# Modulation products of a four-layer diffusion step, in bursts of four feature tiles with a load one burst ahead

## The chip, the cores and the metric

The kernel runs on one core of a Trainium2 chip. The metric is device time in microseconds of one execution; of several runs the median counts. All times below come from the times of the kernel before and from one profiled execution of it.

## What is computed

The reference is one inference step of a four-layer backbone on 512 latent tokens and 128 context tokens, 1024 features wide. Layer i uses another attention (neighbourhood, sliding window, low rank, grouped), and every layer has the same frame. What concerns this case is the adaptive normalisation: each layer takes six vectors of 1024 numbers from a product of the conditioning vector with a 1024 x 6144 matrix.

```python
def adaln(cond, w_mod, b_mod):
    m = jax.nn.silu(cond) @ w_mod + b_mod
    return [t[:, None, :] for t in jnp.split(m, 6, axis=-1)]

def modulate(h, shift, scale):
    return h * (1 + scale) + shift

# a layer, with (shift1, scale1, gate1, shift2, scale2, gate2) = adaln(...)
# x = x + gate1 * mixer(modulate(rms_norm(x, norm1_g), shift1, scale1))
# x = x + gate2 * swiglu(modulate(rms_norm(x, norm2_g), shift2, scale2))
def swiglu(h, w_gate, w_up, w_down):
    return (jax.nn.silu(h @ w_gate) * (h @ w_up)) @ w_down
```

There are two conditioning vectors (latents and context), so the modulation is a product with two rows: little arithmetic, and 24 MB of weights a layer that are read once.

## The kernel before

Activations lie feature-major: eight feature tiles of 128 rows by 640 tokens. The large products are done to float32's accuracy from a high and a low part of each operand: a weight block of 128 x 512 is loaded (`raw`, 256 KB, four places in turn), ScalarE copies its high part (`whi`), VectorE or GpSimd subtracts to get the low part (`wlo`), and TensorE makes three products of each pair. In the feed-forward part the accumulators are called `big`, and the gate and up products go by seven block products (Strassen), whose sums of weights are `sum`. In attention `S` holds the scores, `tp` transposes, and `sm` the rest. `sm` also holds the modulation's accumulator in every phase.

The modulation of the next layer is made as a filler beside other work. The generator `mod_part` makes 4 w columns: for each of the eight feature tiles k it loads a strip of the matrix (128 x 4 w, `rawm`) and makes four products of 32 rows side by side in the array, then it yields; a ninth step copies the accumulator out (`modev`), puts the values into columns with a small product by `sel`, and adds the bias. Layer 0's own columns 2048 to 6144 are made in its attention with w = 128, and their strips lie in the `raw` places of the weights. All others use w = 256, strips of 512 KB in two buffers of their own (`rawm`): layer 1's in the feed-forward part of layer 0, layer 2's in the attention (two thirds) and feed-forward part (one third) of layer 1, layer 3's in the feed-forward part of layer 2. Layer 3 makes none. The first layer's first 2048 columns have a function of their own, `mod_first`, which stays.

Where a step stands in the program is set by `job` and `tick` in attention (so many steps spread over the 16 units) and by `fill` in the feed-forward part: `EDGE` steps after the output product, some after each gate or up product, and the last `EDGE` ones at the end by `flush`. The order on each engine is then set by the tile framework's scheduler, which goes by priority and a simulated timeline: it may draw a later instruction forward where it believes an engine to be idle. All weight, modulation and key loads are issued by SyncE (SP) in one order; `k<-k` copies keys from one half of the partitions to the other, `bias` and `craw` are loads for attention.

A passage that this text calls the edge is the beginning of a feed-forward part: output product, second normalisation (`make_b`, on VectorE, lines 630 to 651), and the first gate and up products. The remainder is called the interior.

Of the kernel before, what the change touches and what calls it, by code (L numbers as in the profile page):

```python
# [37 lines left out]
# feature tiles whose token halves go one after the other at the end of a phase, and steps of modulation kept for there  # L38
LAST, EDGE = 2, 9
# units of attention by which a group's products, normalisation and pairs are ahead  # L40
# [4 lines left out]
# ---------------------------------------------------------------- layout of the weights  # L45
# [5 lines left out]
def weight_plan():  # L51
    """(key, features tiles, columns, builder) of every weight of a product, in the order of use."""
# [59 lines left out]
# columns (one value a partition) and rows (one value a column, the same in every partition)  # L112
# [29 lines left out]
def na_bias(rpb):  # L142
    """Bias and validity of the three kinds of query block: [16 heads, 128 queries, 3, 384]."""
# [24 lines left out]
def to_perm(a):  # L168
    """Latent tokens from (row, column) order to (column // 8, row, column % 8) order, first axis."""
    return a.reshape(8, 8, 8, *a.shape[1:]).swapaxes(0, 1).reshape(a.shape)  # L170
# [89 lines left out]
# ---------------------------------------------------------------- the kernel  # L260
class Net:
# [5 lines left out]
    # -- small helpers  # L267
# [3 lines left out]
    def alt(self, out, in_, share=0.5):  # L271
        """A copy, on the scalar engine for a share of the calls and on the vector engine for the others."""
        self.flip += share
        if self.flip >= 1:
            self.flip -= 1
            self.nc.scalar.copy(out, in_)
        else:
            self.nc.vector.tensor_copy(out, in_)

    def banks(self, kind):  # L280
        """The accumulators of a phase: name -> (banks of each, number)."""
# [8 lines left out]
    def weights(self, key, part=None):  # L290
        """The blocks of a weight, or one of them, on chip in two parts: for each feature tile (high, low) [128, n]."""
# [14 lines left out]
    def two(self, raw, eng):  # L306
        """The two parts of a block."""
# [5 lines left out]
    def slots(self, more):  # L313
        """The places of blocks and of their parts, in turn; the feed-forward phase has some more of them."""
# [23 lines left out]
    # -- the whole  # L338
# [13 lines left out]
    def constants(self):  # L352
        nc, a, cp = self.nc, self.a, self.cp
        # two columns a feature tile: a product takes these and 30 more, whose rows of the result nobody reads
# [22 lines left out]
    # -- modulation: silu(cond) @ w_mod + b_mod, as columns  # L377
# [6 lines left out]
    def mod_first(self, b, pool):  # L384
        """The first layer's shift and scale of feature tiles 2 b and 2 b + 1."""
# [22 lines left out]
    def mod_part(self, L, c0, w, pool, tag=None, bufs=1):  # L408
        """Columns c0 to c0 + 4 w - 1 of the layer's modulation: four products side by side in the array."""
        nc = self.nc  # L410
        mod, moda = self.mod_tiles(L)
        acc = self.ps()
        for k in range(ND):
            raw = pool.tile([P, 4 * w], F32, tag=tag, name=tag, bufs=bufs) if pool else self.slot("raw")
            nc.sync.dma_start(raw, self.a["wmod"][L, k * P:(k + 1) * P, c0:c0 + 4 * w])
            for j in range(4):
                self.mm(acc[32 * j:32 * j + 32, :w], self.cond[:, 2 * k:2 * k + 32], raw[:, j * w:(j + 1) * w], k == 0, k == ND - 1)
            yield
        ev = (pool or self.wp).tile([P, w], F32, tag="modev", name="modev")
# [16 lines left out]
    def mod_parts(self, L, c0, c1, *args):  # L436
        w = args[0]
        self.mod_done[L] = c1
        for c in range(c0, c1, 4 * w):
            yield from self.mod_part(L, c, *args)  # L440

    def fill(self, n):
        """n steps of the work that waits for idle time of the tensor engine."""
# [15 lines left out]
    # -- normalisation  # L459
    def stat(self, pool, d, halves=(0, 1), src=None):  # L460
        """Adds the squares of feature tile d; after the last one, makes 1 / rms of every token."""
# [51 lines left out]
    # -- products  # L513
    def mm3(self, out, x, w, start, stop):
        """out += x.T @ w to float32's accuracy, from parts of 12 bits."""
# [4 lines left out]
    def proj_first(self, key, n, evac):  # L520
        """Token-major product of h, the features outermost: five accumulators of n columns."""
# [13 lines left out]
    def proj(self, key, n, evac):  # L535
        """Token-major product of h, a step for each tile of tokens."""
# [10 lines left out]
    def feat(self, halves, ws, acts, L, i, d):  # L547
        """Feature-major product, x += gate * w.T @ act over the list of feature tiles: halves is {half: bank}."""
# [7 lines left out]
    def halves_first(self, weights, acts, L, i, n, after, step=None):  # L556
        """feat for all feature tiles; for the last n, the first half of the tokens goes first."""
# [14 lines left out]
    def residual(self, L, i, d, halves):  # L572
        """x += gate * y for one feature tile of y, or a half of it: halves is {half: y}."""
# [6 lines left out]
    # -- products by seven block products (Strassen, Winograd's form)  # L580
# [3 lines left out]
    def scaled(self, pool, L, halves, d, raws):  # L584
        """A feature tile of x (or a half of it) by its scale, for make_b."""
# [13 lines left out]
    def make_b(self, pool, L, B, raws):  # L599
        """The second normalisation: the quarters of h that the seven block products take and their sums, all in two  # L600
        parts: B[name] = [(high, low) of feature tile i of the half's four]. A step for each feature tile of the first
# [526 lines left out]


class Full(Attn):  # L1130
    """All the latents against the latents and the cache."""

    def blocks(self, g, pr, hf, u):
        net = self.net
# [598 lines left out]
```

## Time and profile before

| | us |
|---|---|
| median of 3 runs | 3285.33 |
| lowest, highest | 3277.95, 3286.36 |
| span of the profiled execution | 3285.3 |
| TensorE busy with matmuls | 3123.6 |
| VectorE busy | 2155.9 |
| ScalarE busy | 1527.9 |
| GpSimd busy | 1264.1 |

The profiled execution is as long as the median run to a tenth of a microsecond, so terms worked out from it can be set against the median as they stand. In the profile a float32 matmul of the modulation appears as two records, so one step of four products is a row of x8, and four steps together are x32. A matmul's duration overlaps the next one's, so what a group costs is read from the start of the instruction before it to the start of the one behind it. `128*32` is the part of the array that an instruction uses (rows by columns).

### The profile page before, as it was taken

How to read it: one execution, taken by the hardware profiler on the slowest of the kernel's cores; microseconds unless marked ns; L12 is line 12 of the kernel's file. 1: busy time of each engine (PE TensorE's matmuls, PEld its weight loads, DVE VectorE, ACT ScalarE, POOL GpSimd, SP SyncE). 2: the span in 40 equal slices, each digit the busy share in tenths (PEclk: the TensorE clock that was granted, in tenths of full speed). 3: DMA queues.
4: the chain of work that ended last, by engine and by line, in shares of the span. 5: the costliest groups of instructions: out<-in, count | busy, mean ns of one | idle time of the engine just before them, and what ended most of it. 6: DMA issues, size and time to landing. Idle time of an engine off the chain costs nothing. (4 is left out here: it accounts for less than half of the span.)

```text
span 3285.3 us, 58663 instructions
## 1 busy us (share of the span) xinstructions
PE 3123.6 (95%) x22157; PEld 2847.0 (87%) x22157; DVE 2155.9 (66%) x4167; ACT 1527.9 (47%) x3300; POOL 1264.1 (38%) x1175
## 2 busy tenths in 40 slices
PE   8999989999999999999987999999999999899999
PEld 6997879999887788999976778899998878799999
DVE  5554496666576768667668766865765765867665
ACT  4555453433346755334346765433433576534332
POOL 2442362322244444323234545432322553633322
PEclk9998999999999999999998999999999999899999
DMA  7346542433433343222211223423333111122222
GB/s 236 100 119 195 184 155 86 127 104 117 126 122 98 105 135 105 76 84 83 88 45 40 64 64 120 135 86 119 117 102 122 53 32 29 55 87 76 80 82 83
DMA packets 168251, 331.50 MB, mean 101 GB/s; under 512 B 19616, under 2 KB 49696, under 8 KB 167968
## 3 DMA queue, kind: packets, MB, share of 16 engines
q1 hardware_dynamic: 164800, 323.47, 32.6%
q8 instruction: 175, 2.87, 0.4%
q10 hardware_dynamic: 3168, 4.28, 0.4%
q14 instruction: 108, 0.88, 0.1%
HBM read 303.86 MB, written 4.28 MB: 94 GB/s over the span
## 5 line engine op out<-in xcount | busy, mean ns | idle before, releaser
L269 PE MATMUL big<-hh,whi 128*128 128x320 f32 x2720 | 829.9, 315 | 24.7 <-ACT hh L619 8.5
L269 PE MATMUL big<-hl,whi 128*128 128x320 f32 x2720 | 832.1, 312 | 6.7 <-DVE hl L623 4.6
L269 PE MATMUL big<-hh,wlo 128*128 128x320 f32 x2720 | 824.1, 311 | 0.9 <-DVE wlo L310 0.9
L309 ACT CAST whi<-raw 128x512 fp32r<-128x512 f32 (+3 forms) x668 | 387.7, 586 | 674.1 <-PE big L269 431.8
L310 DVE TENSOR_TENSOR wlo<-raw,whi 128x512 fp32r<-128x512 f32 (+1 forms) x504 | 432.5, 862 | 201.6 <-ACT whi L309 198.5
L269 PEld LDWEIGHTS big<-hh,whi 128*128 128x128 f32 x2720 | 508.4, 190 | 53.9 <-DVE sv L696 13.6
L269 PEld LDWEIGHTS big<-hl,whi 128*128 128x128 f32 x2720 | 511.7, 190 | 20.9 <-DVE hl L623 10.8
L269 PEld LDWEIGHTS big<-hh,wlo 128*128 128x128 f32 x2720 | 510.1, 189 | 2.9 <-DVE wlo L310 2.9
L310 DVE TENSOR_TENSOR wlo<-sum,whi 128x512 fp32r<-128x512 f32 x336 | 302.0, 903 | 73.3 <-ACT whi L309 68.4
L309 ACT CAST whi<-sum 128x512 fp32r<-128x512 f32 x352 | 215.8, 618 | 272.5 <-PE big L269 226.4
L269 PE MATMUL big<-al,whi 128*128 128x320 f32 x1408 | 335.9, 311 | 3.2 <-POOL al L582 3.2
L310 POOL TENSOR_TENSOR wlo<-raw,whi 128x512 fp32r<-128x512 f32 (+2 forms) x164 | 223.4, 1374 | 294.4 <-ACT whi L309 266.5
L269 PE MATMUL big<-ah,whi 128*128 128x320 f32 x1408 | 333.8, 312 | 1.2 <-ACT ah L734 1.2
L269 PE MATMUL big<-ah,wlo 128*128 128x320 f32 x1408 | 333.4, 310 | 0.0
L1018 POOL TENSOR_SCALAR p<-p,st 128x640 f32<-128x640 f32 (+2 forms) x256 | 201.2, 790 | 315.7 <-DVE st L1017 227.9
L709 POOL TENSOR_TENSOR y<-y,sv 128x320 f32<-128x320 f32 x132 | 146.7, 1118 | 354.0 <-DVE sv L696 300.8
L670 POOL TENSOR_TENSOR sum<-raw,sum 128x512 f32<-128x512 f32 x88 | 124.0, 1409 | 410.1 <-ACT whi L309 206.2
L670 POOL TENSOR_TENSOR sum<-raw 128x512 f32<-128x512 f32 x88 | 127.5, 1449 | 364.7 <-DMA raw<-in_wall 180.6
L577 DVE SCALAR_TENSOR_TENSOR x<-big,mod,x 128x320 f32<-128x320 f32 (+2 forms) x480 | 182.4, 432 | 117.4 <-PE big L269 116.8
L269 PEld LDWEIGHTS big<-al,whi 128*128 128x128 f32 x1408 | 240.2, 189 | 6.5 <-POOL al L582 3.7
L269 PEld LDWEIGHTS big<-ah,whi 128*128 128x128 f32 x1408 | 238.3, 188 | 8.0 <-issue 2.5
L269 PEld LDWEIGHTS big<-ah,wlo 128*128 128x128 f32 x1408 | 239.6, 189 | 0.2
(264 smaller groups left out, 6169.2 us busy)
## 6 DMA issues: line engine op xcount, KB each, us to landing
raw<-in_wall SPq DMA_DIRECT2D x644, 256.0 KB, 2.7
rawm<-in_wmod SPq DMA_DIRECT2D x144, 512.0 KB, 4.3
raw<-in_wmod SPq DMA_DIRECT2D x96, 256.0 KB, 4.5
k<-k SPq DMA_DIRECT2D x38, 384.0 KB, 4.4
raw<-in_wall SPq DMA_DIRECT2D x96, 128.0 KB, 2.2
bias<-in_nabias SPq DMA_DIRECT2D x16, 576.0 KB, 5.5
qpe<-pes SPq DMA_DIRECT2D x56, 80.0 KB, 2.1
out_y<-x ACTq DMA_DIRECT2D x8, 320.0 KB, 2.2
```

The source lines that it names most:

```text
L269: self.nc.tensor.matmul(out, lhsT=lhsT, rhs=rhs, start=start, stop=stop, skip_group_check=True)
L309: self.nc.scalar.copy(hi, raw)
L310: eng.tensor_tensor(lo, raw, hi.bitcast(F32), ALU.subtract)
L577: self.last = self.nc.vector.scalar_tensor_tensor(xs, halves[b][:, p0:p1], self.mcol(L, i, d, c), xs, ALU.mult, ALU.add)
L670: eng.tensor_tensor(raw[n], raw[x], raw[y], op)
L709: nc.gpsimd.tensor_tensor(y, y, v, ALU.mult)
L1018: nc.gpsimd.tensor_scalar(p, p, rd, 1.0, ALU.mult, ALU.mult)
```

## The change

`mod_parts` no longer loads a strip inside each step. It keeps a list of bursts, each of four feature tiles of one group of 1024 columns. `mod_load` issues the four loads of the next burst into four buffers `rawm`; a step then makes all 16 products of the burst that is on chip, issues the next burst's four loads into the same buffers, and yields. The second burst of a group goes on to the copy and the bias in the same step. So a group of 1024 columns takes two steps in place of nine, and there is one more step at the very start that only loads. Layer 0's columns are now made with w = 256 in buffers of the attention's pool, so they no longer use the weights' `raw` places, and their products are 256 columns wide in place of 128. `EDGE` goes from 9 to 2, and the counts of steps are adapted. A setting that shrinks a scratch area of DMA descriptors makes room for the buffers.

```diff
-LAST, EDGE = 2, 9
+LAST, EDGE = 2, 2
+MODW, BURST = 256, 4
...
-    def mod_part(self, L, c0, w, pool, tag=None, bufs=1):
-        nc = self.nc
+    def mod_part(self, L, c0, pool):
+        nc, w = self.nc, MODW
         mod, moda = self.mod_tiles(L)
         acc = self.ps()
-        for k in range(ND):
-            raw = pool.tile([P, 4 * w], F32, tag=tag, name=tag, bufs=bufs) if pool else self.slot("raw")
-            nc.sync.dma_start(raw, self.a["wmod"][L, k * P:(k + 1) * P, c0:c0 + 4 * w])
-            for j in range(4):
-                self.mm(acc[32 * j:32 * j + 32, :w], self.cond[:, 2 * k:2 * k + 32], raw[:, j * w:(j + 1) * w], k == 0, k == ND - 1)
-            yield
-        ev = (pool or self.wp).tile([P, w], F32, tag="modev", name="modev")
+        for k0 in range(0, ND, BURST):
+            raws = self.mod_raw.pop(0)
+            for k, raw in zip(range(k0, k0 + BURST), raws):
+                for j in range(4):
+                    self.mm(acc[32 * j:32 * j + 32, :w], self.cond[:, 2 * k:2 * k + 32], raw[:, j * w:(j + 1) * w], k == 0,
+                            k == ND - 1)
+            self.mod_load(pool)
+            if k0 + BURST < ND:
+                yield
+        ev = pool.tile([P, w], F32, tag="modev", name="modev")
...
-    def mod_parts(self, L, c0, c1, *args):
-        w = args[0]
+    def mod_load(self, pool):
+        if self.mod_todo:
+            L, c, k0 = self.mod_todo.pop(0)
+            raws = []
+            for k in range(k0, k0 + BURST):
+                raws.append(pool.tile([P, 4 * MODW], F32, tag="rawm", name="rawm", bufs=BURST))
+                self.nc.sync.dma_start(raws[-1], self.a["wmod"][L, k * P:(k + 1) * P, c:c + 4 * MODW])
+            self.mod_raw.append(raws)
+    def mod_parts(self, L, c0, c1, pool):
         self.mod_done[L] = c1
-        for c in range(c0, c1, 4 * w):
-            yield from self.mod_part(L, c, *args)
+        cs = range(c0, c1, 4 * MODW)
+        self.mod_todo, self.mod_raw = [(L, c, k0) for c in cs for k0 in range(0, ND, BURST)], []
+        self.mod_load(pool)
+        yield
+        for c in cs:
+            yield from self.mod_part(L, c, pool)
...
-                todo = (6144 - c0) // 1024 * 9 - 2 * EDGE
-                self.filler = [self.mod_parts(L + 1, c0, 6144, 256, fp, "rawm", 2)]
+                todo = (6144 - c0) // (4 * MODW) * (ND // BURST) + 1 - 2 * EDGE
+                self.filler = [self.mod_parts(L + 1, c0, 6144, fp)]
...
-                self.job(net.mod_parts(2, 0, 4096, 256, self.ap, "rawm", 2), 36, 0, 16)
+                self.job(net.mod_parts(2, 0, 4096, self.ap), 9, 0, 16)
...
-            self.job(net.mod_parts(0, 2048, 6144, 128, None), 72, 7, 16)
+            self.job(net.mod_parts(0, 2048, 6144, self.ap), 9, 7, 16)
...
-    nc = bacc.Bacc("TRN2", target_bir_lowering=False, num_devices=1)
+    nc = bacc.Bacc("TRN2", target_bir_lowering=False, num_devices=1, dynamic_dma_scratch_size=1024)
```

On TensorE, in the last down product of layer 0's feed-forward part, where the trace of before has a wait at 881 us, the order before has two steps together between products by `ah` and `al` (the gated activations' parts):

```order
L269 MATMUL big<-ah,whi 128x320
L269 MATMUL big<-al,whi 128x320
L269 MATMUL big<-ah,wlo 128x320
L269 MATMUL big<-ah,whi 128x320 x6
L269 MATMUL sm<-rawm,cond 32x256 x8
L269 MATMUL big<-al,whi 128x320 x2
L269 MATMUL big<-ah,wlo 128x320 x2
```

and after, at the tenth of the twelve bursts of that part, the four steps of a burst stand in one row:

```order
L271 MATMUL big<-hh,whi 128x320
L271 MATMUL big<-hl,whi 128x320
L271 MATMUL big<-hh,wlo 128x320
L271 MATMUL sm<-rawm,cond 32x256 x16
L271 MATMUL big<-ah,whi 128x320 x2
L271 MATMUL big<-al,whi 128x320 x2
```

What moved is that 16 products stand between the same two large ones, where there were 8.

On SP, in the second half of layer 0's attention, loads of single strips before (`raw<-in_wmod`, in the weights' places) alternate with weights, biases and key copies:

```order
L299 DMA raw<-in_wall 128x512
L415 DMA raw<-in_wmod 128x512 x6
L299 DMA raw<-in_wall 128x512
L415 DMA raw<-in_wmod 128x512 x3
L1298 DMA bias<-in_nabias 128x1152
L299 DMA raw<-in_wall 128x512
L415 DMA raw<-in_wmod 128x512 x2
L983 DMA k<-k 64x1536 x2
L1298 DMA bias<-in_nabias 128x1152
```

and after:

```order
L301 DMA raw<-in_wall 128x512 x2
L448 DMA rawm<-in_wmod 128x1024 x4
L1317 DMA bias<-in_nabias 128x1152
L448 DMA rawm<-in_wmod 128x1024 x2
L301 DMA raw<-in_wall 128x512
L448 DMA rawm<-in_wmod 128x1024
L1002 DMA k<-k 64x1536 x2
L1317 DMA bias<-in_nabias 128x1152
```

What moved is that strips of twice the size go in rows of up to four, and weights have their places to themselves.

At the edge of layer 0's feed-forward part SP has before:

```order
L415 DMA rawm<-in_wmod 128x1024 x3
L665 DMA raw<-in_wall 128x512 x2
L415 DMA rawm<-in_wmod 128x1024
L665 DMA raw<-in_wall 128x512
L415 DMA rawm<-in_wmod 128x1024 x8
L665 DMA raw<-in_wall 128x512
L415 DMA rawm<-in_wmod 128x1024 x2
```

and after:

```order
L448 DMA rawm<-in_wmod 128x1024 x4
L684 DMA raw<-in_wall 128x512
L448 DMA rawm<-in_wmod 128x1024
L684 DMA raw<-in_wall 128x512
L448 DMA rawm<-in_wmod 128x1024
L684 DMA raw<-in_wall 128x512
L448 DMA rawm<-in_wmod 128x1024 x12
L684 DMA raw<-in_wall 128x512
```

What moved is that more strips stand at the edge, up to 12 in a row without a weight between them.

## Rows read from the trace of the kernel before

**Rows 1.** The page's first part: engine, busy us (share of the span), instructions.
```profile
PE 3123.6 (95%) x22157; PEld 2847.0 (87%) x22157; DVE 2155.9 (66%) x4167; ACT 1527.9 (47%) x3300; POOL 1264.1 (38%) x1175
```

**Rows 2.** Windows: attention of layer 0, interior, attention of layer 1, interior of layer 2.
```profile
core 0: us, PE busy (x) PEld busy (x) DVE busy (x) ACT busy (x) POOL busy (x), PEclk, DMA share, GB/s
...
240.00:391.00 151.00, 137.62 (x1366) 114.16 (x1365) 66.68 (x200) 70.88 (x188) 38.98 (x58) 0.92 0.59 184
...
480.00:910.00 430.00, 426.44 (x2962) 405.66 (x2960) 268.47 (x442) 154.68 (x284) 127.87 (x92) 1.00 0.35 110
910.00:1183.00 273.00, 260.08 (x1953) 212.27 (x1949) 187.13 (x526) 163.54 (x454) 118.80 (x141) 0.98 0.34 106
...
2090.00:2518.00 428.00, 424.44 (x2955) 405.89 (x2954) 268.92 (x443) 153.79 (x285) 128.87 (x94) 1.00 0.35 108
```

**Rows 3.** The tile `rawm` over the whole span: ns min/median/max, first and last start.
```profile
L269 PE MATMUL sm<-rawm,cond x1152: 379/379/637, 415.7 to 2517.5; 128*32 128x256 f32 x192
...
DMA to landing us min/median/max: 3.4/4.3/7.8
```

**Rows 4.** Timeline of TensorE, layer 0's interior (start, length): two steps, one step.
```profile
701.39 0.31 PE L269 MATMUL big<-hh,wlo 128*128 128x320 f32 x1
701.63 1.07 PE L269 MATMUL sm<-rawm,cond 128*32 128x256 f32 x16
702.63 0.42 PE L269 MATMUL big<-hh,whi 128*128 128x320 f32 x1
...
863.17 0.31 PE L269 MATMUL big<-hl,whi 128*128 128x320 f32 x1
863.32 0.31 PE L269 MATMUL big<-hh,wlo 128*128 128x320 f32 x1
863.56 0.64 PE L269 MATMUL sm<-rawm,cond 128*32 128x256 f32 x8
864.13 0.56 PE L269 MATMUL big<-ah,whi 128*128 128x320 f32 x2
```

**Rows 5.** Timeline of TensorE, layer 0's attention: four steps of 128 columns, one step.
```profile
276.52 1.08 PE L269 MATMUL sm<-raw,cond 128*32 128x128 f32 x32
...
290.46 0.43 PE L269 MATMUL sm<-raw,cond 128*32 128x128 f32 x8
```

**Rows 6.** TensorE's waits (us, times, longest) in 240:391, 480:910, 910:1183, 2090:2520.
```profile
PE sm L269 <- DMA raw<-in_wmod: 6.7, 7, 1.9
...
PE sm L269 <- DMA rawm<-in_wmod: 3.0, 2, 2.4
...
PE sm L269 <- DMA rawm<-in_wmod: 2.8, 3, 1.8
...
PE sm L269 <- DMA rawm<-in_wmod: 2.2, 2, 1.7
```

**Rows 7.** Lines 630 and 582 at the edges of layers 2 and 3; window of layer 2's.
```profile
L630 DVE TENSOR_TENSOR raw<-raw,rstd x16: 476/479/1584, 2036.8 to 2063.4; 128x320 f32<-128x320 f32 x16
L582 DVE TENSOR_TENSOR hl<-raw,hh x4: 476/478/1143, 2058.4 to 2069.5; 128x320 fp32r<-128x320 f32 x4
...
L630 DVE TENSOR_TENSOR raw<-raw,rstd x16: 476/480/1582, 2828.6 to 2853.0; 128x320 f32<-128x320 f32 x16
L582 DVE TENSOR_TENSOR hl<-raw,hh x4: 477/1150/1158, 2847.9 to 2862.1; 128x320 fp32r<-128x320 f32 x4
...
2028.00:2086.00 58.00, 49.43 (x372) 36.08 (x371) 53.25 (x88) 35.71 (x77) 34.23 (x27) 0.97 0.65 211
```

**Rows 8.** Windows of layer 0's attention, columns as in Rows 2: full queues, and behind them.
```profile
276.00:280.00 4.00, 4.00 (x57) 3.52 (x55) 2.03 (x9) 2.78 (x9) 0.59 (x1) 1.00 1.05 334
...
304.00:308.00 4.00, 2.96 (x21) 2.52 (x20) 0.42 (x1) 1.86 (x4) 1.28 (x1) 1.00 1.05 248
308.00:312.00 4.00, 2.54 (x22) 1.85 (x20) 1.23 (x3) 0.00 (x0) 0.00 (x0) 1.00 1.06 208
312.00:316.00 4.00, 3.10 (x20) 2.53 (x20) 0.97 (x3) 1.16 (x3) 0.00 (x0) 0.52 0.63 192
316.00:320.00 4.00, 4.00 (x25) 3.50 (x25) 1.51 (x9) 2.45 (x8) 2.72 (x4) 0.50 0.20 68
```

## The prediction

> **What bounds the kernel now.** I read the page first: TensorE is busy with matmuls for 95% of the span, the next engine, VectorE, for 66% [rows 1]. Then the windows by stage. In the interiors of layers 0 and 2, TensorE is busy 426.4 of 430 and 424.4 of 428 us [rows 2]: there is no hole, and whatever it does not have to do shortens the stage. In the two attentions that carry modulation it is idle 13.4 us of 151 (layer 0) and 12.9 of 273 (layer 1) [rows 2]: mostly bound by TensorE, with waits in between. The edges are another case. The second normalisation, from the first product of line 630 to the last subtraction of line 582, takes 2036.8 to 2069.5 = 32.7 us in layer 2, with modulation beside it, and 2828.6 to 2862.1 = 33.5 us in layer 3, which has none; VectorE is busy 53.3 of 58 us there and TensorE 49.4 [rows 7]. So at an edge VectorE sets the time and modulation is free up to the 8 to 9 us that TensorE has left.
>
> Then the modulation itself, which in float32 is 1152 matmul records of `rawm` (a few are missing) and runs from 416 to 2518 us [rows 3]. The timeline tells what a step costs. One step alone: the large product before it starts at 863.32, the one behind at 864.13, 0.81 us apart, where two large ones follow each other after 0.15 us (863.17, 863.32); so the step takes 0.66 us. Two steps in one row: 701.39 to 702.63, 1.24 us, so 1.09 for both [rows 4]. A further step costs 0.43 us, and the going over to the 128 x 32 part of the array and back 0.23 us. For strips of 128 columns, eight records last 0.43 us and 32 last 1.08 us, so a further step costs 0.65 / 3 = 0.22 us [rows 5]; the switch I take as the same 0.23.
>
> **The change, part by part.** *Fewer switches.* I counted in both orders the rows of modulation products that stand between other TensorE instructions, and the steps in them (products over four, rounded up, since a piece of one to three products takes as long as four side by side: a large share of the rows are such pieces, and the bursts are broken up by the scheduler too). Interior of layer 0: 28 rows and 39 steps before, 12 and 26 after: 28 x 0.23 + 39 x 0.43 = 23.2 us before, 12 x 0.23 + 26 x 0.43 = 13.9 after, -9.3. Interior of layer 2: 24 and 33 before, 12 and 26 after: 19.7 to 13.9, -5.8. Attention of layer 1: 33 and 39 before, 25 and 43 after: 24.4 to 24.2, -0.1 (here the bursts are cut into many pieces). Attention of layer 3: a leftover of 0.7 goes. Attention of layer 0, with 0.22 a step before: 45 rows and 73 steps of 128 columns, 26.4 us, to 22 rows and 39 steps of 256 columns, 21.8 us: -4.6. All of this lies on an engine that is full or nearly so. Sum: -20.5 us.
>
> By the Trainium skill, TensorEngine Tiling (Array Packing), Key Properties, a change of the tiling mode drains TensorE; with the drain of some 175 ns that TensorE: Matmul & The Clock Gate gives under Single matmul latency, a switch would be estimated at 0.18 us in place of 0.23, and the sum at some -17 in place of -20.5. The measured 0.23 decides.
>
> *Steps moved to the edges.* Part of the interiors' gain is that work goes to the edges: 18 to 27 steps and 15 to 18 rows in layer 0, 19 to 27 and 16 to 18 in layer 2, 17 to 16 and 14 to 9 in layer 1. On TensorE that is 4.6 + 3.9 - 1.6 = +6.9 us. What hides it is VectorE's chain of the second normalisation, which took the same 33 us with and without modulation, and TensorE's 8.6 idle us in 58 [rows 7]. The loads: some eight strips more of 0.52 MB each add 4.2 MB to 211 GB/s x 58 us = 12.2 MB, together 283 GB/s; the queues have moved 334 GB/s [rows 8]. So I charge 0, and 6.9 us if the cover is gone.
>
> *Waits for strips.* TensorE itself waits for modulation strips 6.7 us in layer 0's attention, 3.0 in layer 0's interior, 2.8 in layer 1's attention and 2.2 in layer 2's interior [rows 6]. Two buffers and a landing of 4.3 us (3.4 to 7.8) [rows 3] leave little lead. With a burst ahead a strip has the time between two bursts: in layer 0's interior the closest pair is 56 large products apart, 56 x 0.146 = 8.2 us, and 2.1 MB at 334 GB/s take 6.3 us. So these waits can go. But a wait can also come back, since four loads wait together for the same burst on SP. Bounds for the four: all 14.7 us gained, or as much lost again. In the two interiors, whose loads have few neighbours (DMA share 0.35 [rows 2]), I take 3 of the 5.2; in the attentions, where weights and key copies go through the same queue, 1.3 of 9.5. Sum -4.3.
>
> *SP.* Every burst has four loads that wait for TensorE to have read the buffers; behind them on SP wait weights, biases and key copies. The number of bytes is the same, and before, too, each load waited for a matmul and had the same neighbours; in layer 0's attention weights now have their own places, which can only help them. I charge 0, and the price if this is wrong is the second rival. *The rest:* the small products, the copies and the bias stay; in layer 0 their number halves, off the path. The accumulator `sm` is held over two steps in place of nine: not priced, and in the lower end of the range.
>
> Sum: -20.5 + 0 - 4.3 = -24.8 us. The profiled execution took 3285.3 us, as much as the median, so the forecast is **3260 us**.
>
> **The rivals.** *Everything goes.* If all waits for strips go as well, it is -20.5 - 14.7, and with the idle time and low clock behind some of them (0.50 for 4 us after the long waits of layer 0's attention [rows 8]) some 6 more: -41, 3244 us. For it: four loads in flight in place of two. Against: VectorE or a weight is often late next.
>
> *The queue jams, and it is slower.* In layer 0's attention the queues are full from 304 to 312 us (share 1.05 and 1.06, 248 and 208 GB/s), TensorE idles 1.0, 1.5 and 0.9 us in three slices of 4 us, and then runs at a clock of 0.52 and 0.50, the lower of its two levels (1.2 GHz), for 8 us [rows 8], which loses half of what it could have done in them: 3.4 + 4.0 = 7.4 us for one jam, and some 10 with a slow slice more on either side. Such a jam comes where strips, a bias and key copies are asked for at once, and a burst puts 2.1 MB in front of them in one piece. There are 16 bursts in the two attentions that carry modulation. Were five of them to jam anew, it would be -24.8 + 50 = +25, 3310 us. It decides from three and a half new jams (35 us, 10 over the gain). DMA: Bandwidth & Descriptors of the Trainium skill, Queues, rings and completion order, says that descriptors of one ring are consumed in order, so a small copy issued behind a burst waits for it; that is the mechanism here, and the full slices agree with it. Against: the same bytes went through the same queue before, and layer 1's attention has a DMA share of 0.34 [rows 2].
>
> *It comes to nothing.* The edges are not covered (+6.9), the waits only move to other places (0), and in the attentions the switches saved are swallowed by waits on softmax: -9.3 - 5.8 + 6.9 = -8 us, 3277 us. For it: the idle 13 us in each attention show that TensorE is not alone on the path there.
>
> That the change does not do what it says, because the scheduler cuts the bursts up, is in the counts above; in layer 1's attention it is the case.
>
> **How the numbers follow.** Forecast (3250 to 3272) 0.60; everything goes 0.12; comes to nothing 0.15; jam 0.13. About 0.3%, 10 us, can be told from no change. Faster by more (below 3275.5) are the first two, 0.72; the same is the third, 0.15; slower the jam, 0.13. The range holds the forecast, everything that goes (3243 and up) and the case of nothing up to its uncovered end, 3288; the jam is left out.
>
> **What would show it.** In the profile after: in the interiors rows of x32 at 2.0 us in place of x8 at 0.66, their stretches some 9 and 6 us shorter; the waits for `rawm` there gone; the edges as long as before, line 630 to line 582 in 33 us. Layer 0's attention 5 to 8 us shorter, layer 1's as before. I am wrong if the edges grow by more than 3 us each (strips too late for the rows of 12 loads), if waits on key copies or weights grow in an attention, or if a stretch of low clock stands behind bursts.

## The result and the profile after

The changed kernel takes 3258.52 us (median; 3253.98 to 3266.37), beside 3286.36 us for the kernel before on the same chip: ratio 0.9917, 95% interval 0.9894 to 0.994. That is 27.8 us less; the forecast was 3260 and 25 less. The profiled execution of the changed kernel took 3255.87 us (its span is 3254.1), 2.7 below the median, so single stages of it are read with care below.

The page's first part, engine, busy us (share of the span) and instructions, answers to [rows 1]:

```profile
PE 3104.7 (95%) x21901; PEld 2843.0 (87%) x21901; DVE 2166.9 (67%) x4166; ACT 1527.7 (47%) x3296; POOL 1263.1 (39%) x1175
```

TensorE is busy 18.9 us less, and no other engine has become a bound. The windows by stage (columns as in [rows 2]: attention of layer 0 from 240 us, interior of layer 0, attention of layer 1, interior of layer 2):

```profile
240.00:380.00 140.00, 129.81 (x1077) 103.91 (x1076) 70.27 (x199) 70.37 (x185) 40.89 (x56) 0.95 0.62 194
469.00:884.00 415.00, 412.95 (x2886) 402.39 (x2884) 270.47 (x440) 153.84 (x284) 127.87 (x93) 1.00 0.32 100
884.00:1161.00 277.00, 263.81 (x1946) 216.18 (x1945) 190.95 (x527) 164.56 (x452) 117.03 (x141) 0.97 0.33 104
2068.00:2485.00 417.00, 414.57 (x2891) 403.35 (x2891) 271.12 (x443) 155.44 (x287) 128.57 (x93) 1.00 0.31 100
```

The interiors are still full, and about 14 and 10 us shorter. Layer 1's attention has become no shorter. The tile `rawm` over the whole span (duration in ns; then the idle time of the engine ahead of its instructions in us and times; then issue to landing) answers to [rows 3]; it now includes layer 0's own columns, which were `raw` before. The last line is the idle time of the kernel before, for comparison:

```profile
L271 PE MATMUL sm<-rawm,cond x1408: 376/379/636, 255.5 to 2479.4; 128*32 128x256 f32 x176
...
  DMA rawm<-in_wmod: 5.7, 11
...
DMA to landing us min/median/max: 3.4/5.6/11.9
...
  DMA rawm<-in_wmod: 45.7, 42
```

A strip lands later than before (5.6 us against 4.3), and yet TensorE does not wait for it where it did (5.7 us in place of 45.7, weight loads included). In layer 0's interior alone the median landing is 5.4 us, against 4.0 before; a run below with the same four buffers and single steps has 4.4, so most of the delay goes with four loads being asked for at once. TensorE's waits in layer 0's interior (us, times, longest), which before were 3.0 us for strips [rows 6]:

```profile
PE big L271 <- DVE sv L715: 2.0, 2, 1.8
```

`sv` is a partial result of the block products that VectorE makes; before, that wait was 0.6 us. In layer 2's interior the strips' 2.2 us are gone as well, and 2.2 us for `sv` stand there, where there were 1.2.

A burst in layer 0's interior, on TensorE's timeline (start, length), answers to [rows 4]:

```profile
842.14 0.31 PE L271 MATMUL big<-hl,whi 128*128 128x320 f32 x1
842.29 0.31 PE L271 MATMUL big<-hh,wlo 128*128 128x320 f32 x1
842.53 1.93 PE L271 MATMUL sm<-rawm,cond 128*32 128x256 f32 x32
844.39 0.56 PE L271 MATMUL big<-ah,whi 128*128 128x320 f32 x2
```

From the start ahead (842.29) to the start behind (844.39) it is 2.10 us; less the 0.15 that two large products are apart, four steps cost 1.95 us. The prices of the prediction give 0.23 + 4 x 0.43 = 1.95. (It is the burst whose order stands ahead of the prediction. That order and the one of the kernel before are from different places of the stage, so the large products around them are not the same two.)

The edges of layers 2 and 3 (VectorE, first and last start) and a window that begins 9 us before line 649 in layer 2, as that of [rows 7] does before line 630:

```profile
L649 DVE TENSOR_TENSOR raw<-raw,rstd x16: 476/482/1587, 2012.1 to 2039.6; 128x320 f32<-128x320 f32 x16
...
L601 DVE TENSOR_TENSOR hl<-raw,hh x4: 476/480/1145, 2034.6 to 2046.0; 128x320 fp32r<-128x320 f32 x4
...
L649 DVE TENSOR_TENSOR raw<-raw,rstd x16: 477/481/1582, 2797.0 to 2820.7; 128x320 f32<-128x320 f32 x16
...
L601 DVE TENSOR_TENSOR hl<-raw,hh x4: 477/479/1142, 2815.0 to 2828.2; 128x320 fp32r<-128x320 f32 x4
...
2003.00:2061.00 58.00, 52.29 (x419) 37.92 (x419) 51.02 (x87) 34.58 (x73) 33.55 (x27) 0.94 0.73 258
```

The chain of the second normalisation takes 33.9 us with the added modulation and 31.2 without (32.7 and 33.5 before). TensorE is busy 52.3 of 58 us in place of 49.4: it did the extra steps mostly in time that it had. The stage still grew by 2.1 us (table).

For the table I took from TensorE's timeline where the stages begin (first product into `big`, the 400th of them, last; products with `consts` left out), and added for four stages what the rows of modulation took, each from the start of the instruction ahead to the start of the one behind, less 0.133. The time that such a row waited for its strip is in it, and shown apart. Idle time just before the instruction behind a row is in it too: 4.5 us before and 0.8 after in layer 0's attention, 3.3 and none in layer 1's.

| stage, us | before | after | modulation rows before | after |
|---|---|---|---|---|
| attention 0 | 390.9 | 379.8 | 40.6 in 45 (waits 6.7) | 22.9 in 22 |
| edge 0 | 89.4 | 88.9 | | |
| interior 0 | 429.3 | 415.1 | 27.1 in 28 (3.0) | 14.0 in 12 |
| attention 1 | 273.3 | 277.2 | 32.3 in 33 (2.8) | 24.8 in 25 (0.2) |
| edge and interior 1 | 494.7 | 491.6 | | |
| attention 2 | 326.4 | 326.6 | | |
| edge 2 | 87.2 | 89.3 | | |
| interior 2 | 426.0 | 416.2 | 23.4 in 24 (2.2) | 14.0 in 12 |
| layer 3, with its end | 767.9 | 769.4 | | |

Three questions were open after this. Which part of the change gives the gain: the burst (fewer rows), the place of the load in the program (a burst ahead), or the four buffers? Why did layer 1's attention get 3.9 us longer? And is the 11 us of layer 0's attention the change's, where the sum had 4.6 and a share of 1.3?

### The profile page after: what moved, and what is told of

Read it like the earlier page. It is cut to its first block, busy times and chain, and to the rows that moved or that the text cites. A ratio compares the mean times of both kernels' runs of the same rounds, so it can differ in the third digit from the quotient of the medians.

```text
span 3254.1 us, 58089 instructions
## 1 busy us (share of the span) xinstructions
PE 3104.7 (95%) x21901; PEld 2843.0 (87%) x21901; DVE 2166.9 (67%) x4166; ACT 1527.7 (47%) x3296; POOL 1263.1 (39%) x1175
## 5 line engine op out<-in xcount | busy, mean ns | idle before, releaser
L312 DVE TENSOR_TENSOR wlo<-raw,whi 128x512 fp32r<-128x512 f32 (+1 forms) x504 | 444.6, 885 | 202.9 <-ACT whi L311 199.5
```

Of the source, the lines that this page charges most:

```text
L312: eng.tensor_tensor(lo, raw, hi.bitcast(F32), ALU.subtract)
```

## Experiments

Theory: the gain is fewer rows of modulation products, and strips that are there when TensorE comes to them. Rivals: the load ahead alone gives it, whatever the rows; or the buffers alone; and for the attentions, that a pair of profiled executions does not tell what a stage is worth.

**Single steps, with the four buffers and loads four steps ahead.**

```diff
-LAST, EDGE = 2, 2
+LAST, EDGE = 2, 9
-MODW, BURST = 256, 4
+MODW, BURST, DEEP = 256, 1, 4
...
-                raws.append(pool.tile([P, 4 * MODW], F32, tag="rawm", name="rawm", bufs=BURST))
+                raws.append(pool.tile([P, 4 * MODW], F32, tag="rawm", name="rawm", bufs=BURST * DEEP))
...
-            if k0 + BURST < ND:
-                yield
+            yield
...
-        self.mod_load(pool)
+        for _ in range(DEEP):
+            self.mod_load(pool)
```

> The changed kernel with single steps again (one strip, four products, a yield), but with the strips loaded four steps ahead into four buffers of their own, and EDGE back at 9. Counted in its order on TensorE: interiors 19 rows and 28 steps each (changed kernel: 12 and 26), attention of layer 0 31 rows and 39 steps (22 and 39), of layer 1 24 and 38 (25 and 43), edges the same. Theory A (what counts is the number of switches and steps on a full TensorE, 0.23 and 0.43 us): +2.5 in each interior, +2.1 and -2.3 in the attentions, so some 5 us over the changed kernel, about 3263 us. Theory B (what counts is that a strip is there before its step): no difference, 3258. Theory C (the burst as one piece is what brings the gain): most of the 28 us comes back, over 3275.

Measured: 3282.45 us, ratio 0.9981 (0.9968 to 0.9994). Most of the gain is gone, although buffers and lead are those of the changed kernel. This is 16 us more than the burst kernel of the next experiment beside the same runs of the kernel before (3290.67). The number fits the third expectation (over 3275); the price of rows and steps gives 8 us between the two orders, half of it. Rows of products are back: 31 in layer 0's attention in place of 22, and 19 in each interior in place of 12. And so are waits for strips: before products and weight loads of `rawm` 28.9 us in all, where the changed kernel has 5.7. TensorE's waits in layer 0's interior and in layer 1's attention:

```profile
PE big L271 <- DVE sv L715: 2.8, 2, 2.0
PE sm L271 <- DMA rawm<-in_wmod: 1.8, 2, 1.2
```

```profile
PE sm L271 <- DMA rawm<-in_wmod: 4.6, 3, 2.3
PE S L271 <- ACT hh L526: 2.7, 1, 2.7
PE tp L1005 <- ACT pt L278: 2.5, 4, 0.9
```

The profiled execution was the longest of its runs (3294.7), so its stages are not used for sums.

**Bursts, but each burst's loads issued in the step that uses them.** Four buffers, and then the same with two.

```diff
         for k0 in range(0, ND, BURST):
+            self.mod_load(pool)
             raws = self.mod_raw.pop(0)
...
-            self.mod_load(pool)
             if k0 + BURST < ND:
```

> The changed kernel with the four loads issued in the step that uses them, in place of a step ahead; four buffers and bursts of four stay. The order on TensorE is that of the changed kernel in the interiors, at the edges and in the attention of layer 0 (the scheduler draws the loads forward by itself); in the attention of layer 1 it has 20 rows and 38 steps in place of 25 and 43. Theory A: 3.3 us less than the changed kernel, about 3255. Theory B, if the burst ahead in the program is what has the strips there in time: the waits for strips (14.7 us in the kernel before) come back, 3265 to 3272.

> As the kernel with loads in the step, but two buffers in place of four (as many as before the change), bursts of four products in the program. Counted: interiors 21 rows and 28 steps each, edges 19 steps in place of 27 (so steps move from the edges into the interiors: 100 products there in place of 87), attentions 28 and 36 rows and steps in layer 0, 31 and 42 in layer 1. Theory A: 83 us of steps and switches outside the edges in place of 74 in the changed kernel, so +9, about 3268. Theory B adds waits for strips, two in flight for four products: 3270 to 3280. If the buffers did not matter: 3258.

Measured: with four buffers 3266.27 us, 0.9924 (0.991 to 0.9938), which cannot be told from the changed kernel; with two 3303.46, 1.0043 (1.0028 to 1.0058), slower than the kernel before and than every expectation (3258 to 3280). So the load ahead that the program writes out adds nothing: the scheduler draws a load forward as soon as its buffer is free. The tile `rawm` with four buffers, loads not ahead in the program:

```profile
  DMA rawm<-in_wmod: 6.4, 14
...
DMA to landing us min/median/max: 3.6/5.6/11.6
```

These are the waits and landings of the changed kernel (5.7 and 5.6 us). What makes the lead is the number of buffers. With two of them the waits of TensorE and its weight loads for strips come to 94.4 us over the span, more than in the kernel before (45.7); the order differs too, with 9 us more of rows and steps than the changed kernel's by their price, so the 37 us between the two runs are not the waits' alone. TensorE's waits in layer 0's and in layer 1's attention:

```profile
PE sm L271 <- DMA rawm<-in_wmod: 11.3, 10, 2.7
PE S L271 <- DMA k<-k: 8.7, 5, 3.6
```

```profile
PE sm L271 <- DMA rawm<-in_wmod: 6.5, 5, 2.6
PE S L271 <- DVE q L994: 5.2, 3, 2.9
```

**Single steps in the feed-forward parts alone** (attentions in bursts): the edit is the one of the first run, applied where the accumulators are those of the feed-forward part (`BB` is the length that `burst` gives).

```diff
+    def burst(self):
+        return 1 if 'big' in self.kind else BURST
...
-        for k0 in range(0, ND, BURST):
+        for k0 in range(0, ND, BB):
```

> As changed, but in the feed-forward parts single steps with four buffers in place of bursts (attentions in bursts). By the price of steps and rows (19 rows and 28 steps in place of 12 and 26 in each of the two interiors): 2.5 us each, with the waits seen in the run with single steps everywhere (1.8 and 0.9) 8 us more than the changed kernel, ratio 0.994; the interiors some 419 to 423 us in place of 415 and 416. Rival (what the single steps lose, they lose in the attentions): 0.9917 to 0.9925, interiors below 418.

Measured: 3274.60 us, 0.9952 (0.9936 to 0.9968), 10 us more than the changed kernel's 3264.65 beside 3292.99 (0.9917, below), 11 by the ratios. Interior 0 is 421.6 us and interior 2 417.8. The rows of modulation there take 18.3 and 17.1 us, in 19 rows each, in place of 14.0 in 12: +4.3 with 1.5 of waits, and +3.1 with 0.3. So a row fewer is worth what the price says, and single steps bring waits back even with four buffers. The wait of layer 0's interior on the timeline (start, length, idle before):

```profile
862.47 0.64 PE L271 MATMUL sm<-rawm,cond 128*32 128x256 f32 x8 [0.72 <-DMA rawm<-in_wmod]
863.89 0.64 PE L271 MATMUL sm<-rawm,cond 128*32 128x256 f32 x8 [0.78 <-DMA rawm<-in_wmod]
```

It stands in the last down product, where single steps come close together. The stages agree with the median's 10 us only roughly: interior 0 lost 6.5 us and interior 2 about 2, and the profiled execution was the shortest of its six (3265.89 to 3283.65).

The run also tells what is not the bursts'. Beside the kernel before (429.3 and 426.0), the interiors are 7.7 and 8.2 us shorter with single steps; that is 15.9 of the 24.0 us that they gained. With four buffers the strips' waits fall from 5.2 to 1.8 us, and 9 and 8 steps of modulation move to the edges (27 steps at each edge in place of 18 and 19). So in the interiors most of the gain comes with the buffers and the steps that they let go ahead, and the bursts add some 8 to 10 us.

**Bursts with a higher priority in the attentions** (`PRIO` is 200), so that the scheduler cuts them less.

```diff
+            with contextlib.nullcontext() if "big" in self.kind else self.tc.high_priority(offset=PRIO):
-            for k, raw in zip(range(k0, k0 + BURST), raws):
+                for k, raw in zip(range(k0, k0 + BURST), raws):
```

> The changed kernel with the products of a burst given a priority above attention's own work in the attentions of layers 0 and 1, so that the scheduler no longer cuts them to pieces of one to three products: 20 rows and 32 steps in each in place of 22 and 39 (layer 0) and 25 and 43 (layer 1). Theory A: -3.4 and -5.8 us, about 3249. The rival: TensorE is not alone on the path in attention and a piece of modulation that goes first delays scores and the softmax behind them: no gain or a loss there, 3258 or more, with the interiors unchanged.

Measured: 3269.82 us, 0.9941 (0.9925 to 0.9956), not the gain that fewer rows would give. Layer 0's attention took 376.4 us, 3.4 less than in the changed kernel's first profile (within the scatter found below), and layer 1's 286.3, 9 more. TensorE's waits in layer 1's:

```profile
PE S L271 <- DVE q L996: 6.2, 3, 2.9
PE S L271 <- DVE st L1031: 3.2, 2, 2.8
PE sm L271 <- DMA rawm<-in_wmod: 3.2, 3, 1.5
PE S L271 <- ACT hh L527: 2.7, 1, 2.7
PE S L271 <- ACT pp L1070: 2.4, 1, 2.4
```

The changed kernel has 4.2 us for `q`, 1.2 for `st`, 0.2 for strips and none for `pp` there. I read it so: the cut pieces were filling holes. Kept whole, a burst goes ahead of a small product that VectorE or ScalarE needs for the normalisation (`q`, `st`) or the softmax (`pp`), and TensorE waits for them afterwards. The waits fit this; no run takes one such product by itself.

**The changed kernel again, and each attention undone.** In the first undoing layer 0's own columns are made as before (single steps of 128 columns, in the weights' places), in the second layer 1's attention has single steps and two buffers.

```diff
-            self.job(net.mod_parts(0, 2048, 6144, self.ap), 9, 7, 16)
+            self.job(net.old_parts(0, 2048, 6144, 128, None), 72, 7, 16)
```

```diff
-                self.job(net.mod_parts(2, 0, 4096, self.ap), 9, 0, 16)
+                self.job(net.old_parts(2, 0, 4096, 256, self.ap, "rawm", 2), 36, 0, 16)
```

> The changed kernel once more, beside the partial undoings. Both theories: 0.9917 of the kernel before, some 3263 us where that one takes 3290. What it is for is the stages: theory A (each stage's difference is that stage's own) expects layer 0's attention within 2 us of 379.8 and layer 1's within 2 us of 277.2 us again; theory B (single profiled executions scatter by several us a stage) expects one of the two off by more than 3 us.

> Layer 0's own columns as in the kernel before (single steps of 128 columns, strips in the weights' places), all else as changed. Theory A: layer 0's attention gives back the 11.1 us that it gained, to some 391 us, the interiors keep theirs: 11 us more than the changed kernel, ratio to before 0.995. Theory B (only the 4.6 us of fewer steps and rows were gained there, the rest was scatter): 5 us more, ratio 0.993.

> Layer 1's attention as in the kernel before (single steps, two buffers), all else as changed. Theory A: bursts there cost 3.9 us, since a burst keeps a product of the softmax chain waiting; undone, 273.3 us in place of 277.2, ratio 0.9905. Theory B (its products in burst or single cost the same, 24.2 against 23.7 us by the price of steps): as the changed kernel, 0.9917.

Measured, beside 3292.99 for the kernel before: the changed kernel 3264.65, 0.9917 (0.9899 to 0.9935); layer 0's attention undone 3270.36, 0.994 (0.9924 to 0.9956); layer 1's undone 3264.71, 0.9917 (0.9896 to 0.9938). So no worth of layer 1's attention can be told either way, and nothing shows that the 3.9 us of the first pair were the change's; the kernel before with another issuer of its key copies (below) has 276.3 us there in place of 273.3. Layer 0's is worth 5.7 us by the medians (the intervals overlap from 0.9924 to 0.9935), half of the 11 that the pair showed.

Why the pair misled is in the profile of the same kernel again: its layer 0 attention took 391.5 us, 11.7 more than in the first execution, with every TensorE instruction in the same order. Up to layer 0's first product into `big`, TensorE's order is the same in four of the profiled kernels (changed, again, layer 1 undone, single steps in the feed-forward parts). TensorE's waits there for the copies of keys, in these four and last in the kernel before:

```profile
PE S L271 <- DMA k<-k: 7.9, 7, 2.0
```

```profile
PE S L271 <- DMA k<-k: 14.1, 7, 3.3
```

```profile
PE S L271 <- DMA k<-k: 17.5, 7, 4.2
```

```profile
PE S L271 <- DMA k<-k: 6.4, 4, 2.8
```

```profile
PE S L269 <- DMA k<-k: 5.1, 4, 3.0
```

The four attentions took 379.8, 391.5, 393.8 and 377.4 us, in the order of these waits. One place makes half of the difference of the first two. Windows of the changed kernel (columns as in [rows 2]), and then of the same kernel again:

```profile
204.00:208.00 4.00, 4.00 (x32) 3.45 (x31) 1.15 (x4) 2.19 (x6) 1.16 (x2) 1.00 0.61 185
208.00:212.00 4.00, 4.00 (x43) 3.68 (x41) 1.81 (x6) 0.93 (x3) 1.18 (x2) 1.00 0.01 2
```

```profile
204.00:208.00 4.00, 0.81 (x7) 0.60 (x7) 0.01 (x1) 1.23 (x3) 0.00 (x0) 0.87 1.04 182
208.00:212.00 4.00, 4.00 (x19) 4.00 (x20) 0.74 (x4) 1.08 (x3) 1.16 (x2) 0.50 0.54 137
212.00:216.00 4.00, 4.00 (x25) 3.28 (x25) 0.98 (x3) 0.48 (x1) 0.00 (x0) 0.78 0.01 3
```

Again the DMA engines are full (share 1.04), TensorE has 0.81 of 4 us to do, and then its granted clock is 0.50, the lower of its two levels (1.2 GHz): wait and slow stretch together put this execution some 6 us behind. The first burst of layer 0's modulation is multiplied only at 255 us and lay on chip since 67 us, and the next one's loads are issued after that, so no burst has part in this place. The other half of the 11.7 us arises from 286 us on, at key copies that do have strips beside them.

**Both better halves together.** Priority for the bursts in layer 0's attention alone, layer 1's attention as before the change.

```diff
+            with self.tc.high_priority(offset=PRIO) if L == 0 else contextlib.nullcontext():
...
-                self.job(net.mod_parts(2, 0, 4096, self.ap), 9, 0, 16)
+                self.job(net.old_parts(2, 0, 4096, 256, self.ap, "rawm", 2), 36, 0, 16)
```

> Layer 1's attention as in the kernel before, and in layer 0's attention alone the bursts' products have a higher priority for the scheduler (offset 200), so that it leaves them in fewer rows (20 in place of 22, 32 steps in place of 39). Theory A: -3.4 us there as seen in the run with priority in all attentions, -3.9 in layer 1: 7 us less than the changed kernel, ratio 0.9895. Theory B: only the 3.4, 0.9907.

Measured: 3259.88 us, 0.9903 (0.9885 to 0.9922), 4.8 us below the changed kernel. It agrees with the smaller expectation, but the intervals overlap, so it is not shown to beat it.

**Key copies issued by ScalarE in place of SP**, in the changed kernel, in the kernel before and in the mixed one.

```diff
-        self.nc.sync.dma_start(t[o].bitcast(F32), t[r].bitcast(F32))
+        self.nc.scalar.dma_start(t[o].bitcast(F32), t[r].bitcast(F32))
```

> The changed kernel with the copies of keys from one half of the partitions to the other (k<-k, line 1002) issued by ScalarE in place of SP. Theory A (they land late because they stand behind biases, weights and strips in SP's queue): landing below 5 us in place of 6 to 8, TensorE's 16 to 30 us of waits for them in layer 0's attention fall below 8, that attention takes some 375 us in every execution, 10 us less than the changed kernel: ratio 0.989. Theory B (the sixteen DMA engines are full there, whoever asks): the copies land as late and the time stays at 0.9917, or is longer by what ScalarE waits for the keys before it issues.

> The kernel before with the same single edit (key copies issued by ScalarE). If theory A holds, both kernels are free of late key copies, and layer 0's attention in this one less that in the run above is the change's own worth there: 4.6 us of fewer steps and rows plus about 1 for strips by my sum, 11 us by the one pair of profiled executions. In all 27 us more than the run above by either. If theory B holds: as the kernel before, ratio 1.000.

> Key copies issued by ScalarE, bursts with priority in layer 0's attention, layer 1's attention as before the change. Theory A: 0.9903 of the run without ScalarE's issues less 10 us, 0.987. Theory B: 0.990.

Measured, beside 3290.95: changed kernel 3261.43, 0.9907 (0.9888 to 0.9926); kernel before 3299.58, 1.0027 (1.0013 to 1.004); mixed 3262.61, 0.9914 (0.9901 to 0.9927). The queue theory falls: on ScalarE's queue the copies land as late, and TensorE waits as long (11.0 us; the expectation's 16 to 30 add the weight loads' waits to its own 7.9 to 17.5). The copies in layer 0's attention and TensorE's wait for them, then two windows in which two such copies are on their way (issued at 204.0 and 205.2 us):

```profile
L1002 ACTq DMA_DIRECT2D k<-k x16: 468/469/511, 81.7 to 339.9; - x16
...
  PE S L271: 11.0, 6
...
DMA to landing us min/median/max: 3.5/8.4/11.3
```

```profile
204.00:208.00 4.00, 4.00 (x40) 3.80 (x40) 2.58 (x10) 1.92 (x7) 2.03 (x5) 1.00 1.03 310
208.00:212.00 4.00, 1.93 (x21) 1.55 (x18) 0.42 (x1) 1.23 (x3) 0.40 (x1) 1.00 1.02 237
```

The median landing is 8.4 us, 6.4 and 8.3 in the two executions of the changed kernel with SP's queue, and in the kernel before 5.4 with ScalarE's queue and 5.9 with SP's; the sixteen DMA engines are full in the two windows (1.03, 1.02). By the Trainium skill, DMA: Bandwidth & Descriptors, Issuing engines are not separate DMA queues, transfers started by different engines run on the same 16 DMA engines and interleave, and another issuer saves only its own issuing time; these runs agree. As a control of the change the pair serves little, since the copies did not come free: layer 0's attention took 389.5 us in the kernel before and 384.8 in the changed one, 4.7 apart, in one execution each. Why the kernel before got 9 us slower by ScalarE's issues was not followed up.

## Why the prediction was right

*Price of a step and a row: right.* 1.95 us for a burst, as worked out, and 14.0 us of modulation in each interior after, where the sum had 13.9.

*Fewer rows in the interiors: right, a little too small.* Forecast -9.3 and -5.8. Without their waits the rows fell from 24.1 to 14.0 and from 21.2 to 14.0: -10.1 and -7.2. Of the 2.2 more, 1.5 is that in each interior the row that waited ran on slower afterwards, by 0.7 (the one at 881 us took 4.95 us in place of 1.24, of which 2.99 were its waits). Another 0.3 is idle time behind two rows of layer 2. By the prediction's own count, 8.5 of its 15.1 us are work that goes to the edges; the single steps above show that this part needs the buffers and not the bursts.

*Waits for strips: the term that was mis-sized.* I took 3 of the interiors' 5.2 us, and all 5.2 went; of the attentions' 9.5 I took 1.3, and 9.3 went. Windows of the kernel before around them (columns as in [rows 2]):

```profile
880.00:884.00 4.00, 2.38 (x19) 1.09 (x20) 0.00 (x0) 0.00 (x0) 0.61 (x1) 0.77 0.38 102
884.00:888.00 4.00, 4.00 (x24) 4.00 (x24) 1.73 (x5) 1.36 (x2) 1.30 (x1) 0.80 0.71 249
...
2486.00:2490.00 4.00, 1.76 (x20) 1.02 (x22) 0.00 (x0) 0.00 (x0) 3.06 (x3) 0.98 0.59 228
2490.00:2494.00 4.00, 4.00 (x21) 3.19 (x22) 0.37 (x1) 0.52 (x1) 0.00 (x0) 0.59 0.81 260
```

With the waits went the low clock behind them (0.80 and 0.59 for 4 us, 0.8 and 1.6 us lost), and in return VectorE's `sv` is late for 2.4 us more. The interiors so gave 14.2 + 9.8 = 24.0 us where the sum had 18.1. This is the best established part: over the nine profiled kernels whose interiors have the changed one's order on TensorE (changed, again, loads in the step with four buffers, priority in the attentions, both undoings, mixed, and the two changed ones with ScalarE's issues), interior 0 lies between 414.5 and 416.4 and interior 2 between 414.9 and 416.5, but for 418.7 in the run with priority in the attentions; in the two kernels with the old modulation they are 429.3 and 428.7, and 426.0 and 426.3.

*Layer 0's attention: right in size, in part by luck.* Forecast -4.6 and a share of the 1.3 for waits; undone, 5.7. The price of a row holds here too: nearly every row at full clock with no idle time in it or behind it costs within 0.1 us of its price. The 17.7 us by which the rows fell in the table are this 4.6, 6.7 of waits for strips, 3.7 of idle time behind rows, and 2.1 from five rows at a granted clock of 0.50 to 0.81; 0.6 are left. What I had too small (all the strips' waits went) was offset by what I had at nothing: waits for `k<-k` of 6.4 to 17.5 us stand where there were 5.1, and 6.5 in the run with this attention undone.

*Layer 1's attention: right by the medians* (-0.1; 0.1 by the undoing), and again two things cancel that the sum did not have. Its rows fell by 7.5 us, 2.6 of it waits for strips and 3.3 idle time behind rows, and the time went into other waits of TensorE: for `q` 4.2 us in place of 2.8, for `trs` 2.2 in place of 1.0. That no gain was left is the trace's finding, not the sum's.

*Edges charged at nothing: right within some 2 us.* In the nine kernels edge 0 takes 88.9 to 91.1 us (89.4 and 89.7 with the old modulation), edge 2 88.3 to 89.6 (87.2 and 87.7).

*SP charged at nothing, and the jam: a small part of it came.* Two of the eight pairs of key copies in layer 0's attention land later in the changed kernel. In the three kernels that make layer 0's columns as before, the pair issued at 268 to 272 us landed after 4.8 to 6.4 us and the pair at 333 to 338 us after 3.7 to 6.5. In the nine kernels just named, less the one with this attention undone, and in the one with single steps in the feed-forward parts, the same pairs landed after 8.4 to 11.8 and 8.6 to 13.7 us, most of them with up to four strips of 512 KB on their way beside them. (The pair between them landed sooner, after 4.4 to 9.7 in place of 9.3 to 13.0.) TensorE's waits for keys behind 255 us are 0 to 3.3 us in the three and 3.7 to 11.2 in the others. So one of the signs by which I said I would be wrong, growing waits on key copies, did come; it cost some us in all and not 10 a burst. The mechanism that I gave, a copy waiting in one queue's order behind a burst, is not what decides: in another queue the copies were as late. Nor does it need a burst: with single steps and four buffers everywhere these copies were late too (9.4 to 12.5). Whether the strips' double size or the places of their own make them late was not taken apart.

*Everything goes* did not come: the waits for strips in the attentions went, but others took their place. *Comes to nothing* was right for layer 1's attention alone.

## What to carry to other kernels

A small product that uses another part of the array costs its switch once per row, not once per product: count the rows between other instructions, price a row and a step from two gaps of the timeline, and the sum holds on an engine that is full. (That the 0.23 us is the change of the part of the array, and not some other cost of leaving a run of large products, is a reading; no run here separates the two.) Where it also waits, what is saved can go to the next wait, as in the attentions here. Giving a filler enough buffers of its own matters, more than the bursts did in the interiors; where in the program the loads stand does not, if a scheduler draws them forward whenever a buffer is free. And compare a stage that waits for transfers over several executions, or undo the edit and compare medians, before reading a gain or a loss out of one pair of profiles.

## What was not expected of the hardware

The same TensorE order of layer 0's attention took 377.4 to 393.8 us in four executions. Key copies of the same bytes landed after 4.3 and 6.0 us in one and 8.6 and 10.8 in another (issued at 199 to 200 us), with the DMA engines full in both (share 0.97 and 1.07 from 200 to 204 us); the late ones cost TensorE 3.2 us of wait, from 205 us on, and nearly as much again at the lower clock. What makes the engines slower in one execution than in another stays open.
